# Attention times values on one core: eight stores of the output issued as two runs of four instead of four pairs

## The chip, the cores and the metric

One core of one Trainium2 chip runs the whole program. The metric is the device time of one execution in microseconds (us), as median of several. All runs quoted are of the fast state where a state could be told; the other core of the pair was not used by this program.

## The reference

```python
batch, n_heads, seq, head_dim = 8, 12, 1024, 64
# attn_weights (8, 12, 1024, 1024) float32, v (8, 12, 1024, 64) float32
def reference(attn_weights, v):
    return np.einsum('bhqs,bhsd->bhqd', attn_weights, v).astype(np.float32)
```

403 MB of weights and 25 MB of v are read once, and 25 MB are written. There is little arithmetic for each byte.

## The kernel before

The 96 heads are taken four at a time: 24 groups (`NV`). Each group is two units, 48 units in all (`NU`), and each unit is one load of 8.39 MB of float32 weights, cast to bf16 on the way by the DMA. A unit is transposed on PE, copied out of PSUM by VectorE (DVE) and ScalarE (ACT), multiplied with v, transposed back and written by ACT into one of ten output slots. Two weight buffers alternate: the load of unit n+2 may be issued when unit n is transposed.

GpSimd (POOL) issues all weight loads, the later loads of v, and the stores of the first twenty groups. They share one queue and run in its order.

```python
RING = 5                 # pairs of output slots
NO = 2 * RING
HELD_FROM = NV - 8       # 16: from here stores are held to the end
BY_SYNC = NV - 4         # 20: from here SyncE stores
# ...
def load_attn(n):        # unit n
    pieces = [(0, G)] if n < HALVED else [(0, GH), (GH, GH)]
    for g0, gn in pieces:
        pool.dma_start(out=abf[n % 2][...], in_=attn_q[...]
        ).then_inc(s_abf[n % 2] if g0 == 0 else s_second[n], 16)

def store(q, fours, eng, done):          # groups q .. q + fours - 1
    eng.wait_ge(s_out, 2 * (q + fours) + 1)
    at_slot = osb[:, ds(slot(q), fours)]. ...
    eng.dma_start(out=out_2[q // 2] if fours == 2 else out_q[q], in_=...
    ).then_inc(done, 16)

def store_2(q):
    store(q, 2, pool, s_osb[q // 2 % 2] if q < HELD_FROM else s_held)

for n in range(NU - 2):                  # GpSimd's loop
    q, i = n // 2, n % 2
    if i == 0 and q % 2 == 1 and q + 1 < NV:
        # ... wait for the spread of v
        load_v((q + 1) // 2)
    pool.wait_ge(s_t[True], (n + 1) * PER_DVE)   # unit n is transposed
    load_attn(n + 2)
    if i == 0 and q % 4 == 0 and 0 < q <= HELD_FROM:
        store_2(q - 4)
        store_2(q - 2)
for q in range(HELD_FROM, BY_SYNC, 2):
    store_2(q)
```

SyncE (SP) passes on counts: that a load has landed, that v has landed, and that stores have landed and slots are free. It has part of this written out and part in a loop:

```python
def relays_of(four, eight, stored):
    for n in range(4):
        relay(s_half, s_abf[n % 2], four + 16 * (2 + n // 2))
        if n == 2:
            relay(s_vr, s_v, eight + 16, 2)
            if stored is not None:
                nc.sync.wait_ge(s_osb[0], stored)
                relay(s_free, s_osb[1], stored, 2)
# two relays_of written out, a loop of four rounds with two each, one more written out
```

At the start SyncE loads the first 2.10 MB of v as float32 into output slots, and VectorE casts it as its first work of size:

```python
for two, p0, pn in ((0, 0, P), (1, 0, 96), (1, 96, 22), (1, 118, 10)):
    nc.sync.dma_start(out=v32_2[...], in_=v_2[0][...]).then_inc(s_v0, 16)
# VectorE:
nc.vector.wait_ge(s_v0, 16 * 4)
nc.vector.tensor_copy(out=vr..., in_=v32).then_inc(s_vr, 2)
```

Of the kernel before, what the change touches and what calls it, by code (L numbers as in the profile page):

```python
# [10 lines left out]
def kernel(  # L11
# [18 lines left out]
    nc = tc.nc  # L30
# [16 lines left out]
    NV = NH // VH  # L47
    NU = 2 * NV



    HELD_FROM = NV - 8
    BY_SYNC = NV - 4

# [5 lines left out]
    def slot(q):  # L60
        return q % NO
# [20 lines left out]
    with tc.tile_critical(no_gpsimd_drain=True):  # L82
        sem = tc.alloc_semaphore
# [17 lines left out]
        s_abf = [sem(f"s_abf{i}") for i in range(2)]  # L101
        s_second = {n: sem(f"s_second{n}") for n in range(HALVED, NU)}
        s_v0, s_v = sem("s_v0"), sem("s_v")
        s_osb = [sem(f"s_osb{i}") for i in range(2)]
        s_held, s_end = sem("s_held"), sem("s_end")

        s_t = {True: sem("s_t_dve"), False: sem("s_t_act")}
        s_sp = [sem("s_sp_dve"), sem("s_sp_act")]
# [9 lines left out]
        s_memset, s_const, s_vr = sem("s_memset"), sem("s_const"), sem("s_vr")  # L118

        s_half, s_free = sem("s_half"), sem("s_free")  # L120
# [193 lines left out]
        pool = nc.gpsimd  # L314

        def load_attn(n):
            pieces = [(0, G)] if n < HALVED else [(0, GH), (GH, GH)]
            for g0, gn in pieces:
                pool.dma_start(  # L319
                    out=abf[n % 2][:, ds(g0, gn)].rearrange("p g s -> p (g s)"),  # L320
                    in_=attn_q[n // 2][:, ds((n % 2 * G + g0) * S, gn * S)],
                ).then_inc(s_abf[n % 2] if g0 == 0 else s_second[n], 16)

        def load_v(iv):
            pool.dma_start(  # L325
                out=vr.rearrange("p two b x -> p two (b x)"), in_=v_2[iv]
            ).then_inc(s_v, 16)

        def store(q, fours, eng, done):
            eng.wait_ge(s_out, 2 * (q + fours) + 1)  # L330
            at_slot = osb[:, ds(slot(q), fours)].rearrange("p n r d -> p n (r d)")
            eng.dma_start(  # L332
                out=out_2[q // 2] if fours == 2 else out_q[q],
                in_=at_slot if fours == 2 else at_slot[:, 0],
                **({"single_packet": True} if eng is pool else {}),
            ).then_inc(done, 16)

        def store_2(q):
            store(q, 2, pool, s_osb[q // 2 % 2] if q < HELD_FROM else s_held)

        load_attn(0)
        load_attn(1)
        pool.wait_ge(s_memset, 2)
# [21 lines left out]
        for n in range(NU - 2):  # L365
            q, i = n // 2, n % 2
            if i == 0 and q % 2 == 1 and q + 1 < NV:
                for s in s_sp:
                    pool.wait_ge(s, 2 * q + 2)
                load_v((q + 1) // 2)  # L370
            pool.wait_ge(s_t[True], (n + 1) * PER_DVE)
            load_attn(n + 2)
            if i == 0 and q % 4 == 0 and 0 < q <= HELD_FROM:
                store_2(q - 4)
                store_2(q - 2)
        for q in range(HELD_FROM, BY_SYNC, 2):
            store_2(q)
        pool.drain()


# [10 lines left out]
        def relay(to, of, n, by=1):  # L391
            nc.sync.wait_ge(of, n)
            nc.sync.sem_inc(to, by)

        def relays_of(four, eight, stored):

            for n in range(4):
                relay(s_half, s_abf[n % 2], four + 16 * (2 + n // 2))
                if n == 2:
                    relay(s_vr, s_v, eight + 16, 2)  # L400
                    if stored is not None:
                        nc.sync.wait_ge(s_osb[0], stored)
                        relay(s_free, s_osb[1], stored, 2)

        for i in range(2):
            relay(s_half, s_abf[i], 16)
        for t in range(2):
            relays_of(32 * t, 16 * t, None)
        with nc.Fori(1, HELD_FROM // 4 + 1, 1, engines=(mybir.EngineType.SP,)) as it:
            stored = nc.sync.snap(it * 16)  # L410
            for k in range(2):
                four, eight = (nc.sync.snap(it * (2 * x) + k * x) for x in (32, 16))
                relays_of(four, eight, stored if k == 0 else None)
        for t in range(HELD_FROM // 2 + 2, NV // 2 - 1):
            relays_of(32 * t, 16 * t, None)
        for n in range(HALVED, NU):
            relay(s_half, s_second[n], 16)
        store(NV - 4, 2, nc.sync, s_end)
# [5 lines left out]
        for k in range(2):  # L424
            nc.sync.wait_ge(s_fin[k], 1)
            js = ds(4 * k, 4)
            nc.sync.dma_start(out=outs[:, 1, :, js], in_=rows[:, 1, :, js]).then_inc(s_end, 16)
        for k in range(2):
            nc.sync.wait_ge(s_osb[k], 16 * (HELD_FROM // 4))
        nc.sync.wait_ge(s_held, 16 * (BY_SYNC - HELD_FROM) // 2)  # L430
        nc.sync.wait_ge(s_end, 16 * 5)

# [29 lines left out]
```

## Time and profile before

| | before |
|---|---|
| time, median of the first 3 runs | 1054.05 us (1054.01 to 1055.6) |
| span of the profiled execution | 1052.8 us |
| DMA, busy share | 9 tenths or more in 39 of 40 slices |
| bytes through HBM | 453 MB, 430 GB/s |
| PE busy | 727 us (69%) |
| interval between two units' starts | 19.32 us plain, 24.22 with a load of v, 29.3 to 29.5 with a pair of stores |

How to read it: in the PE timeline each line is a unit's transposes, with its start, its length and, in brackets, how long PE had idled and what ended that. If a load ended it, the start of the line is the moment that the load's last byte was announced, so the differences of such starts are a ledger of what the DMA queue did. The prediction shows these lines for the first pair of stores.

Between unit 2 and unit 45, the last whole load, lie 32 plain intervals and 11 with v: 32 x 19.324 + 11 x 24.22 = 884.8 us (19.324 is the plain interval to one more digit). Whatever a profile has over that is what the loop's eight stores cost.

### The profile page before, as it was taken

The page shows a single profiled execution, that of the slowest core. Times are in us where ns is not written, and L with a number is a line of the kernel's source. Part 1 is how long each engine was busy: PE and PEld are TensorE (multiplying, and loading weights), DVE is VectorE, ACT ScalarE, POOL GpSimd, SP SyncE. Part 2 cuts the span into 40 slices and gives each one's busy share as a digit, 9 for nine tenths or more (in the row PEclk, how much of TensorE's full clock was granted, in tenths as well). Part 3 has the DMA queues.
Part 4 walks back from the last instruction along what each step waited for, and adds up shares of the span by engine and source line. Part 5 has one row for each costly group of instructions (what it writes and reads, how often), then busy time and mean ns, then how long its engine had stood idle before and what let it go on. Part 6 is the DMA issues. An engine that isn't in the chain of part 4 may idle for free.

```text
span 1052.8 us, 16564 instructions
## 1 busy us (share of the span) xinstructions
PE 727.1 (69%) x6920; PEld 681.4 (65%) x6920; DVE 388.3 (37%) x582; ACT 410.1 (39%) x493; POOL 44.9 (4%) x80
## 2 busy tenths in 40 slices
PE   0787778674696587567857658776746866865894
PEld 0776677564686586556856557676746766865884
DVE  0443344332353253233523324433423433532542
ACT  0444345332353353233533334443424433533552
POOL 1000000000000000000000000000000000000000
PEclk9989789788798898789989878898878987987897
DMA  9999999999999999999999999999999999999998
GB/s 236 223 220 209 218 213 218 218 260 245 230 217 204 221 218 296 219 219 218 219 209 212 300 217 219 218 219 219 287 216 218 217 211 225 219 207 231 204 217 337
DMA packets 14329, 240.18 MB, mean 228 GB/s; under 512 B 1269, under 2 KB 1781, under 8 KB 4725
## 3 DMA queue, kind: packets, MB, share of 16 engines
q0 software_dynamic: 12912, 233.84, 99.0%
q1 hardware_dynamic: 1413, 6.29, 1.5%
q8 instruction: 2, 0.03, 0.0%
q14 instruction: 2, 0.02, 0.0%
HBM read 427.82 MB, written 25.17 MB: 430 GB/s over the span
## 4 chain that ended last, share of the span: by engine, by line
DMA 76%; PE 21%; issue 1%; DVE 0%; SPq 0%; ACT 0%; POOL 0%; DVEq 0%
DMA abf<-in_attn_weights_dram 74%; PE bank L130 20%; DMA osb<-in_v_dram 3%; PE bank L172 1%; PE bank L157 0%; DVE vbf L230 0%; SPq L386 0%; PE bank L145 0%; DVE at L251 0%; DVE osb L237 0%; ACT ot L263 0%; POOL abf L319 0%; DVEq L250 0%; DVE vr L309 0%; DVEq L284 0%
## 5 line engine op out<-in xcount | busy, mean ns | idle before, releaser
L130 PE MATMUL bank<-ident,abf 128*128 128x128 f32 x3072 | 443.3, 314 | 283.6 <-DMA abf<-in_attn_weights_dram 278.2
L130 PEld LDWEIGHTS bank<-ident,abf 128*128 128x128 f32 x3072 | 433.4, 214 | 296.8 <-DMA abf<-in_attn_weights_dram 290.1
L251 DVE COPY at<-bank 128x1024 bf16<-128x1024 bf16 x480 | 319.8, 689 | 465.5 <-PE bank L130 464.1
L251 ACT COPY at<-bank 128x1024 bf16<-128x1024 bf16 x288 | 288.6, 1012 | 419.3 <-PE bank L130 419.3
L172 PE MATMUL bank<-at,vbf 128*64 128x256 bf16 x3072 | 215.0, 278 | 0.0
L172 PEld LDWEIGHTS bank<-at,vbf 128*64 128x64 bf16 x3072 | 196.8, 108 | 13.4 <-DVE at L251 4.0
L263 ACT COPY ot<-bank 128x512 f32<-128x512 f32 x48 | 28.1, 586 | 174.2 <-PE bank L172 174.2
L263 DVE COPY ot<-bank 128x512 f32<-128x512 f32 x48 | 33.2, 692 | 151.3 <-PE bank L172 151.3
L157 PE MATMUL bank<-ident,ot 128*128 128x128 f32 x392 | 52.2, 276 | 32.9 <-DVE vbf L230 32.2
L157 PEld LDWEIGHTS bank<-ident,ot 128*128 128x128 f32 x392 | 43.4, 141 | 45.0 <-DVE vbf L230 44.0
L237 ACT COPY osb<-bank 128x512 f32 (+1 forms) x97 | 52.2, 589 | 27.1 <-PE bank L157 26.2
L319 POOL DMA_DIRECT2D abf<-in_attn_weights_dram x50 | 27.2, 544 | 707.9 <-PE bank L130 706.8
L230 DVE CAST vbf<-bank 128x512 bf16<-128x512 f32 x48 | 30.9, 686 | 6.6 <-PE bank L145 6.6
L230 ACT CAST vbf<-bank 128x512 bf16<-128x512 f32 x48 | 25.8, 589 | 11.9 <-PE bank L145 11.9
L145 PE MATMUL bank<-vr,spread 32*128 32x512 bf16 x384 | 25.8, 377 | 0.0
L325 POOL DMA_DIRECT2D vr<-in_v_dram x11 | 7.7, 703 | 238.2 <-PE bank L145 238.2
L251 ACT ACT_TABLE_LOAD x12 | 15.4, 1283 | 1.3 <-SPq L82 1.1
L145 PEld LDWEIGHTS bank<-vr,spread 32*128 32x128 bf16 x384 | 10.0, 92 | 6.8
L309 DVE CAST vr<-osb 128x4096 bf16<-128x4096 f32 x1 | 2.3, 2294 | 28.5 <-DMA osb<-in_v_dram 28.5
L332 POOL DMA_DIRECT2D out_dram<-osb x10 | 7.2, 719 | 12.4 <-ACT osb L237 12.4
L356 POOL TENSOR_SCALAR_AFFINE_SELECT spread<-spread 32x512 bf16<-32x512 bf16 x4 | 2.5, 628 | 0.6
L237 DVE COPY osb<-bank 128x512 f32<-128x512 f32 x1 | 0.7, 692 | 3.1 <-PE bank L157 3.1
(8 smaller groups left out, 2.1 us busy)
## 6 DMA issues: line engine op xcount, KB each, us to landing
abf<-in_attn_weights_dram POOLq DMA_DIRECT2D x46, 4096.0 KB, 31.6
out_dram<-osb POOLq DMA_DIRECT2D x10, 2048.0 KB, 33.9
vr<-in_v_dram POOLq DMA_DIRECT2D x11, 1024.0 KB, 13.2
abf<-in_attn_weights_dram POOLq DMA_DIRECT2D x4, 2048.0 KB, 23.8
out_dram<-osb SPq DMA_DIRECT2D x1, 2048.0 KB, 14.0
osb<-in_v_dram SPq DMA_DIRECT2D x1, 1024.0 KB
out_dram<-osb SPq DMA_DIRECT2D x1, 1024.0 KB, 15.9
osb<-in_v_dram SPq DMA_DIRECT2D x1, 768.0 KB
```

What stands on the lines that cost most here:

```text
L130: last = pe.matmul(out=pt[g % 4][:, k], lhsT=words[:, k], rhs=ident, is_transpose=True, start=(k == 0), stop=(k == KW - 1),)
L145: last = pe.matmul(out=ps, lhsT=spread[rows, b], rhs=vr[rows, two, b], start=(b == 0), stop=(b == VB - 1),)
L157: last = pe.matmul(out=ps[:, ds(j * P, P)], lhsT=ot[:, j0 + j], rhs=ident, is_transpose=True, start=(j == 0), stop=(j == jn - 1),)
L172: last = pe.matmul(out=outs, lhsT=vbf[:, 2 * kw + par, h], rhs=at[:, ds(half * GH, GH), kw, ds(h * VP, VP), par], start=(n == 0), stop=(n ...
L230: copy(out=vbf[:, :, h], in_=ps.rearrange("p (k d) -> p k d", k=SB)).then_inc(s_vbf[e])
L237: return copy(out=rows.rearrange("p (half j) d -> p j half d", half=2)[:, ds(j0, jn)], in_=ps[:, ds(0, jn * P)].rearrange("p (j half d) -> ...
L251: ins = copy(out=at[:, g].rearrange("c k j two -> c (k j two)"), in_=bank[g % 4].bitcast(bf16),)
L263: copy(out=ot.rearrange("c j (h p) -> c h j p", h=VH)[:, ds(2 * e, 2)], in_=po[e].rearrange("c (h j p) -> c h j p", h=2, j=GH),).then_inc( ...
L319: pool.dma_start(out=abf[n % 2][:, ds(g0, gn)].rearrange("p g s -> p (g s)"), in_=attn_q[n // 2][:, ds((n % 2 * G + g0) * S, gn * S)],).th ...
L325: pool.dma_start(out=vr.rearrange("p two b x -> p two (b x)"), in_=v_2[iv]).then_inc(s_v, 16)
L332: eng.dma_start(out=out_2[q // 2] if fours == 2 else out_q[q], in_=at_slot if fours == 2 else at_slot[:, 0], **({"single_packet": True} if ...
L356: pool.affine_select(out=spread[ds(h * VP, VP)], in_=spread[ds(h * VP, VP)], compare_op=mybir.AluOpType.not_equal, fill=1.0, base=0, patte ...
```

## The change

Its intent is fewer turns between reading and writing: the stores of eight heads (2.10 MB) go out four back to back, twice, in front of the held ones. GpSimd now frees the slots itself, and so SyncE's words for the loads fit into one loop.

```diff
+    BURST = 8
...
-        s_osb = [sem(f"s_osb{i}") for i in range(2)]
-        s_held, s_end = sem("s_held"), sem("s_end")
+        s_osb, s_held, s_end = sem("s_osb"), sem("s_held"), sem("s_end")
...
             load_attn(n + 2)
-            if i == 0 and q % 4 == 0 and 0 < q <= HELD_FROM:
-                store_2(q - 4)
-                store_2(q - 2)
+            if i == 0 and q % BURST == 0 and 0 < q <= HELD_FROM:
+                for k in range(q - BURST, q, 2):
+                    store(k, 2, pool, s_osb)
+            if i == 1 and q % BURST == 1 and 1 < q:
+                pool.wait_ge(s_osb, 16 * (q // 2))
+                pool.sem_inc(s_free, BURST // 2)
...
-        for t in range(2):
-            relays_of(32 * t, 16 * t, None)
-        with nc.Fori(1, HELD_FROM // 4 + 1, 1, ...) as it:
-            ...
-        for t in range(HELD_FROM // 2 + 2, NV // 2 - 1):
-            relays_of(32 * t, 16 * t, None)
+        with nc.Fori(1, NV // 2, 1, ...) as it:
+            four, eight = (nc.sync.snap(it * x) for x in (32, 16))
+            for n in range(4):
+                relay(s_half, s_abf[n % 2], four + 16 * (n // 2))
+                if n == 2:
+                    relay(s_vr, s_v, eight, 2)
```

More of the change, by code (lines that the diff above doesn't have):

```diff
@@ L336, in store @@
             ).then_inc(done, 16)
-        def store_2(q):
-            store(q, 2, pool, s_osb[q // 2 % 2] if q < HELD_FROM else s_held)
         load_attn(0)
@@ L372 @@
             load_attn(n + 2)
-            if i == 0 and q % 4 == 0 and 0 < q <= HELD_FROM:
-                store_2(q - 4)
-                store_2(q - 2)
+            if i == 0 and q % BURST == 0 and 0 < q <= HELD_FROM:
[4 more added lines that the diff above has]
+                pool.sem_inc(s_free, BURST // 2)
         for q in range(HELD_FROM, BY_SYNC, 2):
-            store_2(q)
+            store(q, 2, pool, s_held)
         pool.drain()
@@ L393, in relay @@
             nc.sync.sem_inc(to, by)
-        def relays_of(four, eight, stored):
-            for n in range(4):
-                relay(s_half, s_abf[n % 2], four + 16 * (2 + n // 2))
-                if n == 2:
-                    relay(s_vr, s_v, eight + 16, 2)
-                    if stored is not None:
-                        nc.sync.wait_ge(s_osb[0], stored)
-                        relay(s_free, s_osb[1], stored, 2)
         for i in range(2):
             relay(s_half, s_abf[i], 16)
-        for t in range(2):
-            relays_of(32 * t, 16 * t, None)
-        with nc.Fori(1, HELD_FROM // 4 + 1, 1, engines=(mybir.EngineType.SP,)) as it:
-            stored = nc.sync.snap(it * 16)
-            for k in range(2):
-                four, eight = (nc.sync.snap(it * (2 * x) + k * x) for x in (32, 16))
-                relays_of(four, eight, stored if k == 0 else None)
-        for t in range(HELD_FROM // 2 + 2, NV // 2 - 1):
-            relays_of(32 * t, 16 * t, None)
+        with nc.Fori(1, NV // 2, 1, engines=(mybir.EngineType.SP,)) as it:
+            four, eight = (nc.sync.snap(it * x) for x in (32, 16))
[3 more added lines that the diff above has]
+                    relay(s_vr, s_v, eight, 2)
         for n in range(HALVED, NU):
@@ L427 @@
             nc.sync.dma_start(out=outs[:, 1, :, js], in_=rows[:, 1, :, js]).then_inc(s_end, 16)
-        for k in range(2):
-            nc.sync.wait_ge(s_osb[k], 16 * (HELD_FROM // 4))
+        nc.sync.wait_ge(s_osb, 16 * (HELD_FROM // 2))
         nc.sync.wait_ge(s_held, 16 * (BY_SYNC - HELD_FROM) // 2)
```

## The prediction

> **What bounds the kernel now.** I read the page's list of DMA queues first, then the chain of waits, then the table of waits, then the PE and POOL timelines around one pair of stores.
>
> The page's slice row, its DMA part and the chain:
>
> ```profile
> DMA  9999999999999999999999999999999999999998
> ...
> q0 software_dynamic: 12912, 233.84, 99.0%
> ...
> HBM read 427.82 MB, written 25.17 MB: 430 GB/s over the span
> ...
> DMA 76%; PE 21%; issue 1%; DVE 0%; SPq 0%; ACT 0%; POOL 0%; DVEq 0%
> ```
>
> The 16 DMA engines are busy in every slice, and almost all of it is the one queue that GpSimd fills (loads of the attention weights, loads of v, and ten of the stores). 427.82 + 25.17 = 453 MB cross in 1052.8 us. The chain names DMA for 76% and PE for 21%, but the PE pieces in it are the 8 to 10 us of transposes after which GpSimd issues the next load. They are on the chain only because the chain is followed through the issue; the queue holds other work meanwhile. The table of waits says the same:
>
> ```profile
> POOL abf L319 <- PE bank L130: 706.8, 35, 35.8
> ...
> PE bank L130 <- DMA abf<-in_attn_weights_dram: 278.2, 45, 28.9
> ...
> POOL out_dram L332 <- ACT osb L237: 12.4, 4, 3.1
> ```
>
> PE waits for a load 45 times and 278 us in all; GpSimd, which issues, idles for over 700 us. No line has ACT waiting for a store, so the ring of output slots is never short now.
>
> The PE timeline gives the price of each transfer, because a unit that starts with "idle before <-DMA" starts when its load has landed:
>
> ```profile
> 212.26 8.02 PE L130 MATMUL bank<-ident,abf 128*128 128x128 f32 x64 [1.21 <-DMA abf<-in_attn_weights_dram]
> ...
> 231.58 9.78 PE L130 MATMUL bank<-ident,abf 128*128 128x128 f32 x64 [6.03 <-DMA abf<-in_attn_weights_dram]
> ...
> 261.03 10.33 PE L130 MATMUL bank<-ident,abf 128*128 128x128 f32 x64 [11.82 <-DMA abf<-in_attn_weights_dram]
> ...
> 285.25 10.23 PE L130 MATMUL bank<-ident,abf 128*128 128x128 f32 x64 [8.60 <-DMA abf<-in_attn_weights_dram]
> ```
>
> A load alone: 231.58 - 212.26 = 19.32 us. With two stores ahead of it: 261.03 - 231.58 = 29.45. With a load of v ahead of it: 285.25 - 261.03 = 24.22. So a pair of stores costs 29.45 - 19.32 = 10.13 us here and a load of v 4.90. The same subtraction at the three later pairs (units that start at 406.10 and 435.43, 580.49 and 609.83, 754.89 and 784.24) gives 10.01, 10.02 and 10.03. The four pairs cost 40.19 us together.
>
> The POOL timeline of that pair:
>
> ```profile
> 203.49 0.53 POOL L319 DMA_DIRECT2D abf<-in_attn_weights_dram  x1 [25.93 <-PE bank L130]
> 204.01 0.71 POOL L332 DMA_DIRECT2D out_dram<-osb  x1
> 207.82 0.72 POOL L332 DMA_DIRECT2D out_dram<-osb  x1 [3.10 <-ACT osb L237]
> 220.58 0.55 POOL L319 DMA_DIRECT2D abf<-in_attn_weights_dram  x1 [12.03 <-PE bank L130]
> ```
>
> The stores are issued at 204 and 208, when the load that lands at 212.26 is under way and the one issued at 203.49 is still to come. That one lands at 231.58 (28.1 us after issue), and only then do the stores move bytes. The queue is at no time empty there.
>
> **What the Trainium skill says.** "DMA: Bandwidth & Descriptors", section "Where 436 GB/s comes from", puts the ceiling of the 16 ports at 435.2 GB/s. A load reads 128 x 16384 float32 = 8.39 MB; in 19.32 us that is 434.2 GB/s. The trace agrees, and there is no bandwidth left to find. "HBM Reference", section "Access", says that a core streaming alone gets well above its per-core share, about 425 GB/s, bounded by its DMA engines; the 430 GB/s of the page agrees. "DMA: Bandwidth & Descriptors", section "Anatomy of one DMA", gives each DMA a fixed cost of about 2.0 us, mostly the wait for the last write's receipt. In this stream the trace does not show it as lost time: a v load of 2.10 MB costs 4.90 us where 2.10 MB at 434.2 GB/s is 4.83. So joining stores saves no fixed cost of that size. The same page, section "Why a DMA increments its semaphore by 16 and not by 1", warns that two DMAs in flight on one semaphore can fill each other's count. The changed kernel has four on one, but waits for the total of all issued, 64 and then 128, which only complete stores can make.
>
> **The change part by part.**
>
> 1. Stores. Before, GpSimd stores two transfers of eight heads (2.10 MB each) after the load at every fourth group of four heads, four times. After, it stores four at every eighth group, twice. The held two and SyncE's last five are untouched. Bytes are the same: 8 x 2.10 = 16.8 MB. At the load's rate a pair would take 4.19 MB / 434.2 GB/s = 9.66 us, an estimate. It takes 10.02 (10.13 the first time), so the excess is 0.36 to 0.47 a pair, 40.19 - 4 x 9.66 = 1.55 us for all four. Of that, two v loads (9.80) have 0.14 as well without any turn from reading to writing; this part goes with the smaller transfers and stays. What may belong to the turn is 10.02 - 9.80 = 0.22 us, 0.33 the first time. Two turns fewer would save 2 x 0.22 = 0.44 us, at most about 0.55. If the 0.22 goes with the stores themselves, nothing is saved. I take a little over half: 0.3 us.
>
> 2. Pool's issue. Eight stores of 0.72 us each, as before, on an engine that idles 707 us before its loads. Only the last store of a burst has to wait for ACT (3.1 us, as now); the three before it are ready. That makes two such waits in the loop in place of four. Four issues and that wait are about 6 us, and the next load is due about 17 us after the last one (220.58 - 203.49), so no load is issued later. Cost on the path: 0.
>
> 3. The slots. The freeing moves from SyncE to GpSimd: after the load issued in the third unit behind the burst it waits for all stores so far and adds 4 to the free count. By then the load queued behind the stores has landed and been transposed, so the stores have landed too and the wait passes at once. With 5 pairs of slots free at the start, ACT needs the sixth at unit 21; GpSimd gives it after the transposes of unit 19. The tenth is needed at unit 37 and comes at unit 35 (5 + 8 = 13 by then). Both are two units, some 40 us, ahead. Cost 0.
>
> 4. SyncE. Its relays are the same waits and increments in one loop of eleven rounds instead of two unrolled pieces and a loop. They signal second halves, which PE needs 4 us after a unit's start; a loop branch cannot reach the path. SyncE's end has one wait fewer, on stores that landed hundreds of us earlier. Cost 0.
>
> 5. Who starves. During a burst PE has one unit to do. A unit behind a burst lands 19.3 + 20.0 = 39.3 us after the one before, which takes PE some 17.6 us (29.45 - 11.82), so PE idles about 22 us twice instead of about 12 us four times. That is idle time of an engine that is not the bound. Afterwards the next load has been in the queue since the burst, and transposes of 10.4 us leave 9 us before the queue could run dry.
>
> Sum: 1054.05 - 0.3 = 1053.75, told as 1053.7.
>
> **Rivals.**
>
> Turns cost more than I think, or the longer run of writes goes better: for it, the excess of the first pair (10.13). Against it, the whole excess over the load's rate is 1.55 us, and that bounds the gain: 1052.5 at best.
>
> The queue's room becomes the bound: four stores behind two loads are more descriptors than GpSimd has had outstanding in the loop. If there is a limit, the third or fourth issue would last many us instead of 0.72. For it, nothing in this profile; the most seen is two loads and two stores plus a third load. Even then the queue is full while GpSimd waits, so the DMA engines work on. Only if the stall outlived the next load's slack would something be lost: up to 2 us a burst, 1058.
>
> A slot wait takes the place of the removed one: ACT at unit 21 or 37 waits for GpSimd's increment, PE waits for ACT and the next load is late. For it, that the stores land later now, up to 10 us, and are freed in lumps of four pairs. Against it, the order shown in part 3. If it happened once for 20 us beyond the queue's contents, 1060 to 1074.
>
> Long idle slows PE: its granted clock in the stretch from 230 to 235 us is about 0.5 after an idle time of 6 us. After 22 us of idling it may stay low for longer. Even if the 10.3 us became 14, the next load's issue would still fall within the 19.3 us that the queue holds. Cost 0.
>
> **Range and chances.** The gain is held between 0 and 1.55 us by the bytes and the rate, and the three runs of before span 1.6 us, upwards from 1054.0. So 1053.7, with 1052.2 to 1055.5 for 8 in 10. A change over 2% is 21 us. Faster by that is not possible at a load rate that already stands at the ceiling: 0.005. Slower by that needs a blunder in the slot order that I do not see: 0.01. Within 2%: 0.985.
>
> **What would show it.** Right: the DMA row stays at 9 throughout; two PE starts lie about 39.4 us after the one before (19.3 and twice 10.0) instead of four that lie 29.4 after; PE's waits for loads still add up to about 278 us; Pool's store issues stay at 0.72 us, with about 12.4 x 2 / 4 = 6.2 us waited for ACT in all; no line has ACT or POOL waiting for a store. The stores of a burst should land about 33, 38, 42 and 44 us after their issue. If turns matter, a burst costs 19.6 to 19.9 us, not 20.0. Wrong: a start more than 40 us after the one before, a load interval over 19.4 us without v or stores, a store issue of several us, or a DMA slice below 9 in the middle.

## The result, and the profile after

The changed kernel took 1054.17 us (median of 6, 1053.91 to 1054.52), the kernel before 1054.17 us (median of 6, 1053.88 to 1055.6). The ratio is 0.9999, with a 95% interval from 0.9986 to 1.0011: the same.

The page of the changed kernel, its slice row of the DMA engines and its sum of bytes, is that of before to the last digit shown:

```profile
DMA  9999999999999999999999999999999999999998
...
HBM read 427.82 MB, written 25.17 MB: 430 GB/s over the span
```

From its table of waits, the two lines that answer to those of before (us in total, times, longest):

```profile
PE bank L130 <- DMA abf<-in_attn_weights_dram: 280.4, 45, 28.5
...
POOL out_dram L332 <- ACT osb L237: 3.4, 2, 1.7
```

PE waits for loads as often as before and, to 2 us, as long. GpSimd waits for ACT only 3.4 us; no line has GpSimd or ACT waiting for a store. The POOL timeline at the first burst:

```profile
368.99 0.53 POOL L319 DMA_DIRECT2D abf<-in_attn_weights_dram  x1 [25.74 <-PE bank L130]
369.51 2.12 POOL L332 DMA_DIRECT2D out_dram<-osb  x3
373.32 0.71 POOL L332 DMA_DIRECT2D out_dram<-osb  x1 [1.69 <-ACT osb L237]
386.33 0.55 POOL L319 DMA_DIRECT2D abf<-in_attn_weights_dram  x1 [12.29 <-PE bank L130]
```

Four stores are issued in 4.5 us, at 0.7 us each. The queue took them without a stall, and the next load is issued 12.3 us after the last.

Now the ledger. PE's starts in the changed kernel at unit 2, around both bursts, and at unit 45:

```profile
68.57 10.00 PE L130 MATMUL bank<-ident,abf 128*128 128x128 f32 x64 [4.29 <-DMA abf<-in_attn_weights_dram]
...
397.39 9.50 PE L130 MATMUL bank<-ident,abf 128*128 128x128 f32 x64 [6.08 <-DMA abf<-in_attn_weights_dram]
436.27 10.45 PE L130 MATMUL bank<-ident,abf 128*128 128x128 f32 x64 [21.53 <-DMA abf<-in_attn_weights_dram]
...
745.74 9.42 PE L130 MATMUL bank<-ident,abf 128*128 128x128 f32 x64 [6.07 <-DMA abf<-in_attn_weights_dram]
784.63 10.37 PE L130 MATMUL bank<-ident,abf 128*128 128x128 f32 x64 [21.62 <-DMA abf<-in_attn_weights_dram]
...
992.52 8.02 PE L130 MATMUL bank<-ident,abf 128*128 128x128 f32 x64 [1.45 <-DMA abf<-in_attn_weights_dram]
```

And the first and the last of these in the kernel before:

```profile
67.20 10.07 PE L130 MATMUL bank<-ident,abf 128*128 128x128 f32 x64 [4.40 <-DMA abf<-in_attn_weights_dram]
...
992.16 9.43 PE L130 MATMUL bank<-ident,abf 128*128 128x128 f32 x64 [1.94 <-DMA abf<-in_attn_weights_dram]
```

A burst costs 436.27 - 397.39 - 19.32 = 19.56 us, and the second 784.63 - 745.74 - 19.32 = 19.57: together 39.13, where the four pairs of before cost 40.19. So in this one profile the bursts gained 1.06 us, over three times the 0.3 us predicted. But unit 2 started 1.37 us later, and unit 45 starts 0.36 us later than before. Does the change win 1 us in the middle and lose it at the start, or are both numbers accidents of one execution? That is the question for the experiments.

### The profile page after: what moved, and what is told of

It is laid out like the page before. It is cut to its first block, busy times and chain, and to the rows that moved or that the text cites. A ratio compares the mean times of both kernels' runs of the same rounds, so it can differ in the third digit from the quotient of the medians.

```text
span 1052.7 us, 16580 instructions
## 1 busy us (share of the span) xinstructions
PE 723.3 (69%) x6920; PEld 677.5 (64%) x6920; DVE 388.3 (37%) x582; ACT 410.0 (39%) x493; POOL 44.9 (4%) x80
## 3 DMA queue, kind: packets, MB, share of 16 engines
q1 hardware_dynamic: 1413, 6.29, 1.5%
## 4 chain that ended last, share of the span: by engine, by line
DMA 70%; PE 23%; issue 5%; another core or an unknown queue 1%; POOL 0%; DVE 0%; SPq 0%; ACT 0%; DVEq 0%; POOLq 0%
DMA abf<-in_attn_weights_dram 68%; PE bank L130 20%; DMA osb<-in_v_dram 3%; PE bank L172 1%; PE bank L145 1%; PE bank L157 0%; POOL vr L325 0%; DVE vbf L230 0%; SPq L387 0%; POOL abf L319 0%; DVE at L251 0%; DVE osb L237 0%; ACT ot L263 0%; DVEq L250 0%
## 5 line engine op out<-in xcount | busy, mean ns | idle before, releaser
L130 PE MATMUL bank<-ident,abf 128*128 128x128 f32 x3072 | 439.5, 312 | 287.7 <-DMA abf<-in_attn_weights_dram 280.4
```

The costliest lines, as they stand in the source:

```text
L130: last = pe.matmul(out=pt[g % 4][:, k], lhsT=words[:, k], rhs=ident, is_transpose=True, start=(k == 0), stop=(k == KW - 1),)
```

## The experiments

Theory A: a turn from reading to writing costs about 0.22 us on all engines, and the shorter SyncE loop (or something else in the change) makes a late start that eats the gain. Theory B: the late start is of the execution, not of the change; turns cost next to nothing; what a burst seems to cost depends on which of the 16 DMA engines comes last.

### The changed kernel again

No edit.

> The changed kernel once more, unedited. In its first profile the loop's stores cost 39.1 us (two bursts of 19.56) against 40.2 before (four pairs), but the loads of the first three units landed about 1.4 us later than in the profile of before, so nothing came out. Theory 'late start is of the run': the unit starts of this second profile lie at other times, 0 to 2 us away, and the burst costs between 19.5 and 20.1 us, as the engine that ends last differs from run to run. Theory 'late start is of the change' (SyncE's shorter words change the start): unit 8 starts again within 0.3 us of where it did in the first profile of the changed kernel. Time in both: 1054.2, within 0.1% of before.

Measured: 1054.67 us (1054.53 to 1054.72, 5 runs) beside 1054.28 for before (9 runs), ratio 1.0001. The second profile's PE starts at the same units, of which I show unit 2, the first burst and unit 45:

```profile
67.03 9.21 PE L130 MATMUL bank<-ident,abf 128*128 128x128 f32 x64 [6.04 <-DMA abf<-in_attn_weights_dram]
...
396.12 10.12 PE L130 MATMUL bank<-ident,abf 128*128 128x128 f32 x64 [4.65 <-DMA abf<-in_attn_weights_dram]
435.32 9.36 PE L130 MATMUL bank<-ident,abf 128*128 128x128 f32 x64 [21.23 <-DMA abf<-in_attn_weights_dram]
...
992.29 8.02 PE L130 MATMUL bank<-ident,abf 128*128 128x128 f32 x64 [1.34 <-DMA abf<-in_attn_weights_dram]
```

The late start is gone (67.03; unit 8, which the expectation named, starts at 193.05 us instead of 194.30), and so is the gain: the bursts now cost 19.88 and 20.29 us, the second more than the 20.1 that was expected at most. The same code does both. This refutes the part of theory A that blames the change for the late start.

The raw packet records say why the two go together. A packet is the piece of a transfer that one DMA engine moves at a time; its record has a start and a length. The records carry no engine number, but in a run of stores each engine's first packet is recorded at 0.322 us and nearly all others at 0.309, and the packets of an engine follow each other without a gap. So the 16 first packets of a run can be matched with the 16 last ones (times are the record's own, some 10.5 us ahead of the page's):

```text
changed kernel, 1st profile, 1st burst: 64 store packets an engine
  15 engines                           took 19.61 us
  one, which has all 25 long packets   took 20.31 us, ended 425.94
  the one that ended last (one of the 15): began 407.47, 1.2 us after all others, ended 427.08
kernel before, 1st pair: 32 store packets an engine
  15 engines                           took 9.81 us
  one, which has all 10 long packets   took 10.03 us, and ended last of all
```

All engines but one take 9.81 us for a pair and 19.61 for a burst, twice as much to 0.01 us: joining the stores saves nothing. One engine has store packets of 0.324 to 0.38 us. The same match, where it can be made (28 of the 30 pairs and bursts in the profiles of pairs and bursts), leaves one engine over each time: with 9.83 to 10.04 us in a pair, and with 20.29 to 20.31 in each of ten bursts. A load counts as landed when the last of 16 engines is done: behind this burst PE starts 0.36 us after the last engine's last load packet and 1.5 us after the other fifteen. If the engine with the long packets is the last, the interval shows them (10.02 a pair; 20.29 a burst, or 19.88 where it began 0.39 us ahead of the last one). If another engine lags already (here by 1.2 us; that this is the lag of the late start is argued, as no record follows the engine back to it), they hide behind its lag (19.56). The 1.06 us was this.

### Four pairs again, with the rest of the change

```diff
-    BURST = 8
+    BURST = 4
-            if i == 1 and q % BURST == 1 and 1 < q:
+            if i == 1 and q % BURST == 1 and 1 < q <= HELD_FROM + 1:
```

> The stores in four pairs as before, everything else as changed (SyncE's one loop, GpSimd frees the slots). If the bursts save 0.2 us a turn: 0.4 us over the changed kernel, 1054.6. If SyncE's loop costs a late start of 1.4 us and the bursts give it back: 1055.2 to 1055.6. If neither does anything: 1054.2, the same as both, to 0.2 us.

Measured: 1054.15 us (1053.8 to 1054.41, 5 runs) on the same chip, ratio to before 0.9997. It is not slower than the bursts beside it (1054.67). SyncE's loop has no price, and no gain of the bursts shows.

### Eight turns and sixteen

Eight single stores: `BURST = 2` with the same bound on `q`. Sixteen: one store of four heads after every group, each with its own semaphore.

```diff
-            if i == 0 and q % BURST == 0 and 0 < q <= HELD_FROM:
-                for k in range(q - BURST, q, 2):
-                    store(k, 2, pool, s_osb)
-            if i == 1 and q % BURST == 1 and 1 < q:
-                pool.wait_ge(s_osb, 16 * (q // 2))
-                pool.sem_inc(s_free, BURST // 2)
+            if i == 0 and 0 < q <= HELD_FROM:
+                store(q - 1, 1, pool, s_osb[q - 1])
+            if i == 1 and q % 2 == 1 and 1 < q <= HELD_FROM + 1:
+                for k in (q - 3, q - 2):
+                    pool.wait_ge(s_osb[k], 16)
+                pool.sem_inc(s_free, 1)
```

> The same eight stores one at a time, after every second group of four heads: eight turns from reading to writing instead of two. If a turn costs 0.22 us, as the prediction left possible: 6 x 0.22 = 1.3 us over the changed kernel, 1055.5. If a turn costs nothing and the excess belongs to one engine's store packets: within 0.3 us of 1054.2, and each store adds about 4.9 us to the interval between two loads' landings.

> The same bytes as sixteen stores of four heads (1.05 MB each), one after every group of four heads: sixteen turns. If a turn costs 0.22 us: 14 x 0.22 = 3.1 us over the changed kernel, 1057.3. If a DMA has a fixed cost of 2 us that shows: 8 more DMAs, 16 us, 1070. If neither: within 0.4 us of 1054.2.

Measured: eight turns 1055.04 us (1054.93 to 1055.93), sixteen 1055.17 us (1054.99 to 1055.91), 5 runs each, ratios to before 1.0004 and 1.0006. Over the changed kernel on the same chip that is 0.37 us for six more turns and 0.50 us for fourteen more: 0.06 and 0.04 us a turn, against the 0.22 of theory A. Eight more DMAs in the queue cost nothing like a fixed time each either. The expectation for the sixteen (within 0.4 us of 1054.2) missed by half a microsecond, and that for the eight (0.3) likewise, so a turn may not be quite free. These differences lie inside the recorded 95% intervals (about 0.0013 of the time, 1.4 us, either way); only the 3.1 us of theory A for the sixteen lies outside them. (The fixed time of 2 us in that expectation is the page's figure that the prediction cites.) The PE timeline of the eight turns shows where: at units 5 and 6, and 25 and 26,

```profile
129.86 7.95 PE L130 MATMUL bank<-ident,abf 128*128 128x128 f32 x64 [1.73 <-DMA abf<-in_attn_weights_dram]
149.75 10.52 PE L130 MATMUL bank<-ident,abf 128*128 128x128 f32 x64 [6.66 <-DMA abf<-in_attn_weights_dram]
...
567.32 9.48 PE L130 MATMUL bank<-ident,abf 128*128 128x128 f32 x64 [1.95 <-DMA abf<-in_attn_weights_dram]
587.61 10.06 PE L130 MATMUL bank<-ident,abf 128*128 128x128 f32 x64 [5.53 <-DMA abf<-in_attn_weights_dram]
```

the load just ahead of a store took 19.89 and 20.29 us instead of 19.32. In the packet records the load's last packets are held there: at the first turn on all 16 engines, by 0.69 us on average, at the sixth on three, one of them by 0.90 us. A second profile of the kernel before has the same at its first pair (0.68 us on average, on all 16), the first one only on 7. The five profiles of burst kernels have none at their two turns. Why the last load packets wait at some turns, mostly the first, no run here shows.

### Without the loop's stores

The eight stores and the wait for them are left out; the output of the first sixteen groups is wrong.

> The eight stores of the loop are left out (the first sixteen groups of four heads of the output stay wrong on purpose; the slots are freed at the same places). If the loop's stores lie wholly on the path and only their bytes count: 39.2 to 40.2 us less, 1014 to 1015. If part of them was hidden, or if they cost more than the intervals show, the time says by how much: over 1016 or under 1013.

Measured: 1014.3 us (1014.01 to 1014.85, 4 runs) beside 1054.3 (9 runs), ratio 0.9622, so 40.0 us less. Its page still has

```profile
DMA  9999999999999999999999999999999999999998
...
HBM read 427.82 MB, written 8.39 MB: 431 GB/s over the span
```

The stores lie wholly on the path: 16.8 MB less at a rate that stays where it was. At the loads' 434.2 GB/s these bytes alone would take 38.6 us (an estimate), so no order of them could give back more than 1.4 of the 40.0 us.

### The bursts with SyncE's words written out

```diff
-        with nc.Fori(1, NV // 2, 1, ...) as it:
-            ...
+        for t in range(2):
+            relays_of(32 * t, 16 * t)
+        with nc.Fori(1, HELD_FROM // 4 + 1, 1, ...) as it:
+            for k in range(2):
+                four, eight = (nc.sync.snap(it * (2 * x) + k * x) for x in (32, 16))
+                relays_of(four, eight)
+        for t in range(HELD_FROM // 2 + 2, NV // 2 - 1):
+            relays_of(32 * t, 16 * t)
```

> The bursts of the changed kernel with SyncE's words unrolled as before. If SyncE's loop costs a late start of 1.4 us: 1052.8. If SyncE's words do nothing: 1054.2 within 0.2 us.

Measured: 1054.89 us (1054.29 to 1056.95, 5 runs) beside 1054.3, ratio 1.0007, half a microsecond above what was expected if the words do nothing, with one run at 1056.95. Its profile has a late start too (unit 2 at 68.46) with SyncE's words as before, and bursts of 19.57. So the loop is not needed for the late start.

### The kernel before again

> The kernel before once more, one look at its start. Theory 'late start is of the run': unit 8 starts anywhere from 192.4 to 194.5 us and the pairs cost between 9.8 and 10.1 us each. Theory 'late start is of the change': unit 8 starts again at 192.9 within 0.3 us, and the pairs cost 10.0.

Measured: 1054.29 us (one run). Unit 2 starts at 67.12 us; the pairs cost 9.98, 9.82, 9.87 and 9.80, and the held load packets at the first and the last pair 0.82 and 0.17 more: 40.46 in all. Unit 8's start, which the expectation named, agrees with the first profile to 0.1 us, so this run alone does not decide between the theories; the changed kernel's second profile did.

### A third look, on one chip

The changed kernel, the pairs and the eight turns once more, unedited.

> The changed kernel a third time, beside the pairs and the single stores on one chip. Revised theory: the end is set by the last of 16 DMA engines. A turn to stores can hold the last load packet before it (0 to 0.9 us an engine, mostly at the first turn), and in a run of stores one or two engines' packets grow from 0.306 to about 0.33 us once some 6 us of it have passed. Bursts have fewer of the first and more of the second, so: no load packets held before the bursts, about 50 long store packets in the loop, 1054.2 to 1054.9. The prediction's theory (a turn costs 0.22 us on all engines): 0.4 us below the pairs.

> Revised theory: some load packets held before the first pair, 30 to 45 long store packets in the loop, 1053.8 to 1054.7, not above the bursts by more than 0.2 us. The prediction's theory: 0.4 us above the bursts.

> Revised theory: nearly no long store packets (a store alone is over in 5 us), load packets held before the first store on most engines and before some later ones, 0.5 to 1.2 us over pairs. The prediction's theory: 0.9 us over the pairs and 1.3 over the bursts, with the same excess at each of the eight turns, about 0.2 us.

Measured, 5 runs each beside 1054.55 for before (9 runs): bursts 1054.78 (1054.58 to 1054.99), pairs 1054.66 (1054.32 to 1055.94), eight turns 1054.92 (1054.74 to 1055.23); ratios 1.0003, 1.0001, 1.0004. The eight turns are 0.26 us over the pairs and 0.14 over the bursts, below what either theory asked (0.5 to 1.2, or 1.3). The bursts are again not below the pairs. In the loop the bursts had 54 long store packets and no held load packet, the pairs 8 and about 14, the eight turns none and about 60; the count of 8 missed the expected 30 to 45. The pairs' profile fell on the slowest of their five executions, 1055.94 us, and shows a start later than any:

```profile
69.87 9.25 PE L130 MATMUL bank<-ident,abf 128*128 128x128 f32 x64 [4.05 <-DMA abf<-in_attn_weights_dram]
...
408.65 10.31 PE L130 MATMUL bank<-ident,abf 128*128 128x128 f32 x64 [4.61 <-DMA abf<-in_attn_weights_dram]
437.77 9.56 PE L130 MATMUL bank<-ident,abf 128*128 128x128 f32 x64 [10.96 <-DMA abf<-in_attn_weights_dram]
```

Here the pair costs 437.77 - 408.65 - 19.32 = 9.80 us: the excess is gone. Part of it was never there (the 8 long packets make their engine only 0.03 to 0.05 us late in a pair), so this profile alone does not show that a lag hides it.

### An earlier third load

Where does a late start come from? The timelines of the two first profiles, before:

```profile
31.03 2.29 DVE L309 CAST vr<-osb 128x4096 bf16<-128x4096 f32 x1 [28.46 <-DMA osb<-in_v_dram]
...
42.01 0.57 POOL L319 DMA_DIRECT2D abf<-in_attn_weights_dram  x1 [35.79 <-PE bank L130]
```

and of the changed kernel:

```profile
32.72 2.29 DVE L309 CAST vr<-osb 128x4096 bf16<-128x4096 f32 x1 [30.15 <-DMA osb<-in_v_dram]
...
43.50 0.57 POOL L319 DMA_DIRECT2D abf<-in_attn_weights_dram  x1 [37.27 <-PE bank L130]
```

The first v landed 1.7 us later, VectorE, which takes its work in order, began unit 0's copies later, and GpSimd issued the third load at 43.50 instead of 42.01. In the profile with 69.87 it was issued at 45.04, in the second one of the changed kernel at 40.22. Issued after 43 us, it comes too close to the end of the second load (lead engines from about 46 us, by the packet records): engines run dry. Between 45 and 49 us those that had no packet stood idle for 4.7 us, summed over the 16, in the changed kernel's first profile, and 8.8 in the one issued at 45.04; the next packets run up to 1.2 us over their 2.43. The split holds for all fourteen profiles: four issued the third load at 43.50 to 45.04 us, had 0.6 to 8.8 us of such idle time and started unit 2 at 68.17 or later; ten issued it by 42.07, had under 0.05 and started unit 2 by 67.42. In the four the cast of v began at 32.7 us or later, in the eight others with the unedited start by 31.14; why v lands later in some executions no run shows. The landing of v is late because its second half shares the engines with the first weight load. The Trainium skill, "DMA: Bandwidth & Descriptors", section "Queues, rings and completion order", says that an engine goes round its queues packet by packet. Half of v is 8 packets an engine, each behind a load packet of 2.43 us, and the half takes from about 6 us (the first half had landed by 6.29 in the experiment below) to 31.

So I split the first v: VectorE casts the half that lands first, GpSimd the other. (The halves change slots, as ACT writes into one of them in unit 0.)

```diff
-        nc.vector.wait_ge(s_v0, 16 * 4)
-        nc.vector.tensor_copy(out=vr..., in_=v32).then_inc(s_vr, 2)
+        nc.vector.wait_ge(s_v0, 16)
+        nc.vector.tensor_copy(out=vr_h[:, 0], in_=v32_h[0]).then_inc(s_vr)
...
+        pool.wait_ge(s_const, 1 + VH)
+        pool.wait_ge(s_v1, 16 * 3)
+        pool.wait_ge(s_vr, 1)
+        pool.tensor_copy(out=vr_h[:, 1], in_=v32_h[1]).then_inc(s_vr)
```

> The bursts, with the first v loaded in two halves that are waited for apart: VectorE casts the first half alone (it lands before the first attention load), GpSimd the second, so unit 0 no longer waits on VectorE for the whole v. Theory 'the late start comes from unit 0': the third attention load is issued at 36 to 39 us (43.5 in the changed kernel's profile with the late start, 40.2 in one without), unit 2 starts at 67.0 to 67.4 and the loop's stores cost 40.2, the sum that a late start hid: 1054.2 to 1054.7, so the gain of the bursts does not come back. If the late start were the whole loss and bursts did cost 39.1 us by themselves: 1052.8.

> The same edit on the kernel before, with its four pairs. Unit 2 starts at 67.0 to 67.4 in the profile, the pairs cost 40.0 to 40.5: 1053.8 to 1054.3. If the start is still late in this profile (unit 2 after 68.4), the delayed third load is not its cause.

The POOL timeline with bursts:

```profile
30.89 1.89 POOL L366 CAST vr<-osb 128x2048 bf16<-128x2048 f32 x1 [24.68 <-DMA osb<-in_v_dram]
38.66 0.57 POOL L320 DMA_DIRECT2D abf<-in_attn_weights_dram  x1 [5.88 <-PE bank L130]
```

The third load is issued at 38.66 us (39.16 with pairs), and unit 2 starts at 67.04 (67.18): the start is as in the best of the other profiles, though two profiles cannot show that it is never late. It gains no time: bursts 1055.02 us (1054.4 to 1055.34), pairs 1054.42 us (1054.34 to 1055.04), 5 runs each, beside 1054.19 for before (9 runs); ratios 1.0005 and 1.0000. The bursts' own expectation missed twice: the time is 0.3 us above its range, and in the profiled execution, the fastest of the five, they cost 19.59 and 19.85 us without a late start, not 20.1 each: in the first burst an engine that began 0.28 us after the others ended last, and the one with the long packets hid behind it. The pairs are 0.1 us above theirs. Some 0.35 us of both times is outside the span: they are 2.1 to 2.3 us above it, the kernel before beside them 1.8 to 1.9, for a reason that no run shows. No version beats both kernels.

### All profiles in one ledger

Each row is one profiled execution. The third column is unit 45's start less unit 2's less 884.8 us, which includes the loads held at turns and some 0.3 us that single plain intervals have over in some rows.

| profile | unit 2 starts | loop's stores cost | unit 45 starts | its time |
|---|---|---|---|---|
| before | 67.20 | 40.16 | 992.16 | 1054.65 |
| before, again | 67.12 | 40.38 | 992.30 | 1054.29 |
| pairs, one SyncE loop | 67.17 | 39.92 | 991.89 | 1053.80 |
| the same, again | 69.87 | 39.37 | 994.04 | 1055.94 |
| pairs, earlier third load | 67.18 | 39.87 | 991.85 | 1054.54 |
| changed | 68.57 | 39.15 | 992.52 | 1054.52 |
| changed, again | 67.03 | 40.46 | 992.29 | 1054.71 |
| changed, third | 67.30 | 40.16 | 992.26 | 1054.68 |
| bursts, SyncE written out | 68.46 | 39.45 | 992.71 | 1055.13 |
| bursts, earlier third load | 67.04 | 39.74 | 991.58 | 1054.40 |
| eight turns | 66.99 | 42.21 | 994.00 | 1055.93 |
| eight turns, again | 67.23 | 40.90 | 992.93 | 1054.84 |
| sixteen turns | 68.17 | 40.91 | 993.88 | 1055.91 |
| no stores in the loop | 67.42 | -0.05 | 952.17 | 1014.10 |

Bursts and pairs overlap in every column. The three starts after 68.4 go with the three lowest store costs. The ledger stops at unit 45: from there to the end of the span it takes 60.1 to 60.2 us in eight of these profiles and 60.5 to 60.7 in six (the first of before, the pairs with the earlier third load, and all of the bursts but the first). No run shows why, and half a microsecond is as much as lies between bursts and pairs.

## Why the prediction was right or wrong

**The bound, and with it the time: right.** The time lies in the range, at 1054.17 against 1053.7; it would lie there without any gain too, so it tests the bound and not the 0.3 us. That the stores lie wholly on the path of a queue at its ceiling is shown by the run without them: 40.0 us less, where the intervals gave 40.19.

**The gain of 0.3 us: wrong.** The step that failed is in part 1, "What may belong to the turn is 10.02 - 9.80 = 0.22 us". The 0.22 us is real but does not belong to the turn: in the pair followed packet by packet it is one engine's long packets, while the fifteen others took 9.81, and a burst took them 19.61. By the medians of six and fourteen more turns on one chip a turn costs 0.06 and 0.04 us, and 0.02 (0.14 over six) on another, all inside the noise. A sentence further on, "If the 0.22 goes with the stores themselves, nothing is saved", was the case that held. Between kernels on one chip the bursts were 0.52, 0.12 and 0.60 us above the pairs; if that is real, the one engine is a candidate: its long packets (50 to 56 in the loop with bursts, 8 to 41 with pairs) make it about 0.69 us late in a burst, 1.4 in two, and at most 0.23 in a pair, 0.9 in four. That this set the end of those runs is argued and not shown.

**A sign that misled.** The prediction said that if turns matter, a burst costs 19.6 to 19.9 us. The first profile had 19.56, which would have passed for a proof. It was the hiding of one engine behind another. The sign of being wrong, a plain load interval over 19.4 us, did not come in that profile (19.38 at most between whole loads), but once in the second one, 19.63 us between units 2 and 3, at the start and far from any store.

**GpSimd's issue (part 2): right in effect, off in a number.** The wait for ACT was put at 3.1 us a burst, 6.2 in all, and measured 1.7 and 3.4. Three stores are issued before it where there was one, 2.12 us instead of 0.71, and 3.10 - 1.41 = 1.69. Both are idle time of GpSimd.

**Slots and SyncE (parts 3 and 4): right.** No engine waits for a store, and the bursts with SyncE's words written out are at 1054.89, not below.

**Who starves (part 5): right.** Two intervals of 38.88 and 38.89 us (up to 39.61 in the other burst profiles) against 39.3, and PE idle for 21.5 and 21.6 us against 22. PE's sum of waits is 280.4 against 278.

**Rivals.** The queue's room: the four issues took 0.7 us each, so no limit was met. The slot wait: absent. Slow PE after long idling: 10.45 us at most after 21.5 us of idling, with a granted clock of 0.50 in the first 4.7 us of it, where 14 would still have done.

**Landing times.** Predicted 33 to 44 us with a middle of 40; the four of the first burst have a median of 39.0.

**A citation.** The passage on about 425 GB/s stands in "HBM Reference", section "Specifications (TRN2)".

## What to carry to other kernels

In this kernel the queue is busy throughout and moves bytes at the ceiling, and reordering its transfers moved only who idles. In such a case take the ledger of landings first, and price the change by bytes. A landing was that of the last of 16 engines, so a delay of one engine shows or hides by what another one does, and the excess of one interval over another is not a cost that can be divided among its parts. For effects of a few tenths of a microsecond profile the same code two or three times before explaining a difference between two codes.

## What the Trainium skill lacked or had wrong

- "DMA: Bandwidth & Descriptors" has no word on what a turn from loads to stores costs in one queue. Here: the medians differ by 0.02 to 0.06 us a turn, inside the noise; the packets of fifteen engines show none (19.61 us for four stores, 9.81 for two), but at some turns, mostly the first, the load's last packets are held by up to 1.0 us an engine.
- The same page, "Latency and other measured facts", says that engines 7 and 15 are usually slower and guesses at a cause. Here one engine in each run of stores has longer packets, only after some 6 us of the run: 0.324 to 0.38 us instead of 0.309, none or one of them when each store goes alone. The records carry no engine number, so no run shows which engine it is.
- The same page, "Anatomy of one DMA", gives a fixed cost of about 2.0 us a DMA. For transfers queued behind others the runs show none of that size: fourteen more turns with eight more DMAs cost 0.50 us in all.
- "DMA: Bandwidth & Descriptors" describes the arbitration packet by packet, but not what it means for a small load beside large casting loads: the second 1.05 MB of the first v took about 25 us, as each of its packets waits behind one of 2.43 us.
